# Block-diagonal fetch of the chunk inverses and 128-column streams for the small products of a hybrid DeltaNet block

## The chip, the cores and the metric

One core of a Trainium2 chip runs the whole program in one launch. The metric is the device time in microseconds (us), here the median of three runs; the profile is one further execution. The core's engines run side by side: TensorE (PE) multiplies matrices and writes PSUM, VectorE (DVE) and ScalarE (ACT) do elementwise work, GpSimd (POOL) some small operations in SBUF, and SyncE (SP) issues most transfers. PEld is PE's loading of the stationary operand.

## The reference

One transformer-like block over 1024 positions of width 1024, in float32. The part that matters here is the modulation and the chunked gated delta rule of group A, 4 heads of width 128, chunks of 64 positions:

```python
mod = (c_act @ w_ada[l] + b_ada[l])[:, None, :]
shift1, scale1, gate1, shift2, scale2, gate2 = jnp.split(mod, 6, axis=-1)
h = rms_norm(x, norm1_w[l]) * (1.0 + scale1) + shift1
...
lmat = jnp.where(strict, jnp.einsum('bhncd,bhnmd->bhncm', k_beta, k) * decay, 0.0)
tmat = lax.linalg.triangular_solve(lmat, eye, left_side=True, lower=True, unit_diagonal=True)
u = jnp.einsum('bhncm,bhnme->bhnce', tmat, v_beta)
w = jnp.einsum('bhncm,bhnmd->bhncd', tmat, k_beta * jnp.exp(g)[..., None])
```

Then a scan over the chunks, an output projection, and a SwiGLU of width 2816; the last norm ends it.

## The kernel before

The 1024 positions are two halves (`hf` 0 and 1) of 512. The first 500 us or so (input modulation, the combined projection, convolutions, the delta rule, the output projection of the first half) are written as many small tasks, and a planner (`Sim`, L298 to L523) orders their instructions while the program is built: for each instruction it estimates a start from costs (`cost`, L367; transfers from L514) and takes the earliest, with a task's priority (`PR`) breaking near ties. What it decides is the fixed order on every engine's queue; the chip only waits on data. The projection's products (`acc`) have the lowest priority and fill PE between the others. Large products are split into two parts of a rounded type (fp32r), three products each; the small ones run in plain f32, where each product leaves two records of PE in the trace. The rest of the program (from L1493) is in a written order.

Modulation: `ada0` (L625) forms shift1 and scale1 column by column. For each of 8 blocks k of 128 columns it multiplies pieces of the weights (as stationary operand) with one column of `c_act`, or sums made on DVE by `sums0` with one column of ones; `cols0` (L646) reads the result on ACT. A number of pieces per block, `N_PE`, goes to PE: 16 products for block 0, 2 or 4 for the others.

The triangular inverse: per half there are 4 heads x 4 tiles x 2 chunks, each chunk a 64x64 unit triangle. `stage_a` writes the 32x32 diagonal blocks to DRAM (`dl`); `gdn` (L1218) reads them back as 64 rows of 1024 numbers, inverts all 64 at once on DVE (the loop at L1242) and writes the inverses to DRAM (`dx`, L1247). From there ten loads bring them back in three layouts:

- `DD[:, 0]` (tile name qs): blocks stacked one under another, 32 columns wide, two loads of 64 KB on SP
- `xbd[0]` (xbd): blocks on the diagonal of a 128x128 tile for each of 16 tiles, four loads of 64 KB, each on SP or ACT as the planner chooses (`dma2`)
- `XA` (A, cleared by POOL at L1255): blocks at shifted diagonal places, four loads of 32 KB on SP or ACT

DVE turns `DD[:, 0]` round into `DD[:, 1]` (L1262), and then a `merge` (L1178) for each head makes the off-diagonal block of the 64x64 inverse: P (L1185) multiplies the off-diagonal part of L with `DD[:, 1]`, its result is copied back to `DD[:, 0]`, Q (L1192) multiplies that with `XA`, and four copies put Q into `Tt`, which also takes the turned `xbd`. With `Tt` PE forms u (L1204) and w (L1209). P and Q are two products each per head, with a moving operand of 32 columns. Then the scan over the chunks runs (products named K, A and O in the trace).

`ecopy` (L570) is a copy on ACT or DVE, whichever the planner expects to end first.

Of the kernel before, what the change touches and what calls it, by code (L numbers as in the profile page):

```python
# [12 lines left out]
AF = mybir.ActivationFunctionType  # L13
# [4 lines left out]
P = 128  # L18
# [3 lines left out]
DMA_T = (1.8, 0.9)  # L22
D = 1024
KB = 8
# [29 lines left out]
def kernel(  # L54
# [25 lines left out]
    class Ordered:  # L80
# [18 lines left out]
    PE, DVE, ACT, POOL, SP = (Ordered(n, e) for n, e in (  # L99
        ("pe", nc.tensor), ("dve", nc.vector), ("act", nc.scalar), ("pool", nc.gpsimd), ("sp", nc.sync)))  # L100
# [11 lines left out]
    xs, outs = x[0], out[0]  # L112
# [18 lines left out]
    def v3(ap, a):  # L131
        return ap.rearrange("p (a b) -> p a b", a=a)
# [7 lines left out]
    def bc1(row, n):  # L140
        return row.unsqueeze(1).to_broadcast([row.shape[0], n, row.shape[1]])
# [10 lines left out]
    ones = ones_r.bitcast(F32)  # L152
# [39 lines left out]
    def dma(out, in_):  # L192
        SP.dma_start(out=out, in_=in_)

    def dma2(out, in_):
        kw = dict(out=out, in_=in_)
        mover[0].either([("sp", "dma_start", nc.sync.dma_start, (), kw), ("act", "dma_start", nc.scalar.dma_start, (), kw)])
# [37 lines left out]
    c_act = cst.tile([P, KB], F32, name="c_act", tag="c_act")  # L235
# [13 lines left out]
    n1c, bac, n2c, gnc = cols_a[:, 0:8], cols_a[:, 8:56], cols_a[:, 56:64], cols_a[:, 64:65]  # L249
    s1c = cst.tile([P, KB], F32, name="s1c", tag="s1c")  # L250
    b1c = cst.tile([P, KB], F32, name="b1c", tag="b1c")
    nb1 = sp.tile([P, KB], F32, name="nb1", tag="nb1")
# [45 lines left out]
    class Sim:  # L298
# [187 lines left out]
        def run(self):  # L486
            while True:
                self.settle()
                best, cand = None, []
                for task in self.tasks:  # L490
                    r = task["req"]
                    if r[0] != "op":
                        continue
                    starts = [self.start_of(w) for w in r[1]]
                    r[2] = min(range(len(starts)), key=lambda i: starts[i] + r[1][i][1][2] + BIAS.get(r[1][i][0], 0.0))
                    t = starts[r[2]]
                    cand.append((prio(task), t, task["n"], r[1][r[2]], task))
                    if best is None or t < best[0]:
                        best = (t, r[1][r[2]][0])
                if best is None:  # L500
                    late_ = [x["req"] for x in self.tasks if x["req"][0] == "slot" and x["req"][1].slots]
                    if late_:
                        self.now = min(self.data_time(r[2]) for r in late_)
                        continue
                    if self.tasks:
                        raise RuntimeError("stuck: " + "; ".join(f"{x['name']}{x['args'] if x['name'] in ('gdn', 'ab_phase') else ''} {x['req'][0]} {getattr(x['req'][1], 'tag', x['req'][1])}" for x in self.tasks))
                    return
                t0, eng = best
                _, t, _, way, task = min((c_ for c_ in cand if c_[3][0] == eng and c_[1] <= t0 + HOLD.get(eng, 0.0)), key=lambda c_: c_[:3])
                outs, ins, busy, lat, table = way[1]  # L510
                if table:
                    self.table = table
                if lat is None:
                    run_ = min(n_ for n_ in (ap.ap[-1][1] * 4 for ap in outs + ins))  # L514
                    self.pipe = max(t + DMA_T[0], self.pipe) + outs[0].nbytes() / (270e3 if run_ <= 512 else 330e3 if run_ <= 1024 else 380e3)
                    end = rd = self.pipe + DMA_T[1]
                else:
                    end, rd = t + lat, t + busy + 0.1
                self.idle.setdefault(eng, []).append((self.t[eng], t, busy, task["name"], "", outs[0].tensor.name))
                self.t[eng] = t + busy  # L520
                self.now = max(self.now, t)
                self.record("dma" if lat is None else eng, outs, ins, end, rd)
                self.resume(task)  # L523
# [46 lines left out]
    def ecopy(dst, src):  # L570
        sim.either([("act", "copy", nc.scalar.copy, (dst, src), {}), ("dve", "tensor_copy", nc.vector.tensor_copy, (dst, src), {})])
# [9 lines left out]
    def mm(out_, lhsT, rhs, start=True, stop=True):  # L581
        PE.matmul(out_, lhsT, rhs, start=start, stop=stop)
# [28 lines left out]
    acs_ = {}  # L611
# [13 lines left out]
    def ada0():  # L625
        pa_ = bank(chb, "ada")
        for k in range(KB):
            sim.wait(lambda: ("wa", k) in done)
            t = wa[k]
            pa = pa_[:, 2 * k:2 * k + 2]  # L630
            sim.wait(lambda: k == 0 or k in acs_)
            n0 = KB - N_PE[k]
            for s_ in range(2):
                for kk in range(n0, KB):
                    mm(pa[:, s_:s_ + 1], t[:, kk, s_, :], c_act[:, kk:kk + 1], kk == n0, n0 == 0 and kk == KB - 1)
                if n0:
                    mm(pa[:, s_:s_ + 1], acs_[k][:, s_, :], ones[:, 0:1], n0 == KB, True)
            free(t)
            if n0:
                free(acs_[k])  # L640
            sim.spawn(cols0, PR["ada0"], k, pa)
        sim.wait(lambda: all(("cols", k) in done for k in range(KB)))
        free(pa_)
        done.add("ada0")

    def cols0(k, pa):  # L646
        ACT.activation(s1c[:, k:k + 1], pa[:, 1:2], AF.Identity, bias=nb1[:, k:k + 1], scale=n1c[:, k:k + 1])
        ACT.activation(b1c[:, k:k + 1], pa[:, 0:1], AF.Identity, bias=bac[:, k:k + 1])
        done.add(("cols", k))

# [421 lines left out]
    xbd, S = [], {}  # L1072
    sw = lambda ap: ap.rearrange("p t (c n) -> p t c n", c=2)
    tsl = lambda t: slice(t * P, (t + 1) * P)
# [103 lines left out]
    def merge(hf, h, T, XA, DD):  # L1178
        st, t_ = sc_[hf], T[h]
        u = us[hf]  # L1180
        L = t_["L"]
        sim.wait(lambda: ("a", hf, h) in done)
        pP = bank(chb, "P")
        for g in range(2):
            mm(pP[:, 32 * g:32 * g + 32], L[:, 2 * g + 1, :], DD[:, 1, 2 * h + g, :])  # L1185
        ecopy(DD[:, 0, 2 * h:2 * h + 2, :], v3(pP[:, 0:64], 2))
        free(pP)
        Tt = gt("Tt")
        DVE.transpose(flat(Tt), flat(xbd[0][:, 4 * h:4 * h + 4, :]))
        pQ = bank(chb, "Q")  # L1190
        for g in range(2):
            mm(pQ[:, 32 * g:32 * g + 32], XA[:, 2 * h + g, :], DD[:, 0, 2 * h + g, :])  # L1192
        for p in range(2):
            for c in range(2):
                q = 64 * c + 32 - 32 * p
                ecopy(Tt[64 * c:64 * c + 32, p:4:2, 64 * c + 32:64 * c + 64], v3(pQ[q:q + 32, 0:64], 2))
        free(pQ)
        done.add(("q", hf, h))
        DVE.tensor_tensor(t_["L"], t_["kt"], bc2(t_["bk"], P), ALU.mult)
        free(t_["bk"])  # L1200
        sim.wait(lambda: ("vt", hf, h) in done)
        pu = bank(chb, "u")
        for t in range(4):
            mm(pu[:, tsl(t)], Tt[:, t, :], u[:, h, t, :])  # L1204
        ecopy(flat(u[:, h]), pu)
        free(pu)
        pw = bank(chb, "w")
        for t in range(4):
            mm(pw[:, tsl(t)], t_["L"][:, t, :], Tt[:, t, :])  # L1209
        free(t_["L"])  # L1210
        free(Tt)
        ecopy(t_["WQ"].rearrange("p t (c n) -> p t c n", c=4)[:, :, 0:4:3, :],
                 pw.rearrange("p (t c n) -> p t c n", t=4, c=2))
        free(pw)
        DVE.tensor_tensor(t_["kt"], t_["kt"], bc2(st["kd"][:, :, h], P), ALU.mult)
        done.add(("uw", hf, h))

    def gdn(hf):  # L1218
# [4 lines left out]
        dx = drp.tile([64, 1024], F32, name=nm("dx"), tag="dx", bufs=2)  # L1223
# [24 lines left out]
        free(A)  # L1248
        free(tmp)
        DD = gt("qs", (P, 2, 8, 32))  # L1250
        for c in range(2):
            r0 = 32 * c + 16
            dma(DD[64 * c:64 * c + 64, 0], dx[r0:r0 + 16, :].rearrange("(h p) (a b) -> (p a) h b", p=2, a=32))
        XA = gt("A", (P, 8, P))
        POOL.memset(XA, 0.0)  # L1255
        for r in range(4):
            dma2(xbd[0][32 * r:32 * r + 32, :, 32 * r:32 * r + 32], dx[r * 16:r * 16 + 16, :].rearrange("t (a b) -> a t b", a=32))
        for c in range(2):
            for p in range(2):
                q, r0 = 64 * c + 32 - 32 * p, 32 * c + p  # L1260
                dma2(XA[q:q + 32, :, q:q + 32], dx[r0:r0 + 15:2, :].rearrange("t (a b) -> a t b", a=32))
        DVE.transpose(flat(DD[:, 1]), flat(DD[:, 0]))  # L1262
        for h in heads:
            sim.spawn(merge, PR["m"], hf, h, T, XA, DD)
# [9 lines left out]
        for t in range(4):  # L1274
# [3 lines left out]
            for cc in range(2):  # L1278
                r0 = 64 * cc
# [905 lines left out]
```

## Time and profile before

| | |
|---|---|
| runs | 1183.56, 1184.01, 1186.36 us; median 1184.01 |
| profiled execution | 1185.35 us, its span 1183.6 |
| mean granted clock of PE | 0.993 |
| POOL busy | 57.3 us of the span |
| moved by DMA | 207.58 MB, 175 GB/s mean |
| the two merges (P to Q) | from 202.3 and 390.4 us |

How to read it: the span is the time from the first to the last instruction of the profiled execution. Rows of groups give the line, engine, operation, output and inputs by tile name, shape, count, and the time spent. A row of the timeline begins with start and length in us; what stands in brackets is the idle time of that engine ahead of it and what ended it. Most small instructions are recorded with the line of a helper (L442 for all that the planner orders, L91 and L92 for the written order), so tile names are what tells them apart. In rows of stretches the columns are: stretch, its length, busy time (and number of instructions) of PE, PEld, DVE, ACT and POOL, the granted PE clock as a share of full speed, the share of the DMA engines in use, and GB/s.

### The profile page before, as it was taken

How to read it: one execution, taken by the hardware profiler on the slowest of the kernel's cores; microseconds unless marked ns; L12 is line 12 of the kernel's file. 1: busy time of each engine (PE TensorE's matmuls, PEld its weight loads, DVE VectorE, ACT ScalarE, POOL GpSimd, SP SyncE). 2: the span in 40 equal slices, each digit the busy share in tenths (PEclk: the TensorE clock that was granted, in tenths of full speed). 3: DMA queues.
4: the chain of work that ended last, by engine and by line, in shares of the span. 5: the costliest groups of instructions: out<-in, count | busy, mean ns of one | idle time of the engine just before them, and what ended most of it. 6: DMA issues, size and time to landing. Idle time of an engine off the chain costs nothing.

```text
span 1183.6 us, 16666 instructions
## 1 busy us (share of the span) xinstructions
PE 1171.5 (99%) x5657; PEld 982.9 (83%) x5657; DVE 924.8 (78%) x1720; ACT 536.3 (45%) x1174; POOL 57.3 (5%) x92
## 2 busy tenths in 40 slices
PE   8999999999999999999999999999999999999997
PEld 8888888988888888888888888888888888888886
DVE  5998888799988798758787677767767697688676
ACT  4489832458642444225443333333333365433343
POOL 2010000001100001100000000000000000000002
PEclk9999999999999899999999999999999999999999
DMA  9932456544434643722354655455644679869413
GB/s 295 291 95 64 112 161 165 177 117 136 119 103 138 158 149 140 280 86 93 133 175 133 222 190 185 145 178 187 223 152 136 221 278 395 307 202 345 146 42 142
DMA packets 179694, 207.58 MB, mean 175 GB/s; under 512 B 25749, under 2 KB 111898, under 8 KB 179610
## 3 DMA queue, kind: packets, MB, share of 16 engines
q1 hardware_dynamic: 172664, 203.16, 53.4%
q10 hardware_dynamic: 6946, 3.38, 1.1%
q8 instruction: 44, 0.72, 0.2%
q14 instruction: 40, 0.33, 0.1%
HBM read 151.44 MB, written 55.05 MB: 174 GB/s over the span
## 4 chain that ended last, share of the span: by engine, by line
PE 93%; DVE 4%; ACT 1%; DMA 1%; issue 1%; POOL 0%; ACTq 0%; DVEq 0%; POOLq 0%
PE acc L91 34%; PE acc L442 24%; PE dn L91 17%; PE o L91 4%; PE o L442 3%; PE K L442 1%; PE A L442 1%; PE u L442 1%; PE ada L442 1%; PE w L442 1%; DVE xo L92 1%; PE ab L442 1%; PE qk L442 1%; PE kk L442 1%; PE heat L91 1%
## 5 line engine op out<-in xcount | busy, mean ns | idle before, releaser
L442 PE MATMUL acc<-h,u 128*128 128x512 f32 x1200 | 303.4, 400 | 0.0
L442 PEld LDWEIGHTS acc<-h,u 128*128 128x128 f32 x1200 | 220.5, 189 | 41.8
L91 PE MATMUL acc<-h,hl 128*128 128x512 f32 x600 | 140.1, 390 | 0.0
L91 PEld LDWEIGHTS acc<-h,hl 128*128 128x128 f32 x600 | 112.4, 188 | 23.2
L91 PE MATMUL acc<-h,u 128*128 128x512 f32 x456 | 106.1, 389 | 0.0
L91 PE MATMUL acc<-T,hl 128*128 128x512 f32 x432 | 101.3, 390 | 0.2 <-ACT cc L92 0.2
L91 PEld LDWEIGHTS acc<-h,u 128*128 128x128 f32 x456 | 85.6, 188 | 17.8
L91 PEld LDWEIGHTS acc<-T,hl 128*128 128x128 f32 x432 | 80.9, 188 | 17.2 <-ACT cc L92 0.6
L92 DVE TENSOR_TENSOR xo<-xo,dn 128x512 f32<-128x512 f32 x84 | 57.1, 685 | 43.2 <-PE dn L91 34.8
L91 PE MATMUL dn<-h,h 128*128 128x512 f32 x396 | 90.7, 389 | 0.0
L92 ACT COPY cc<-acc 128x512 f32<-128x512 f32 x66 | 38.5, 591 | 108.1 <-PE acc L91 108.1
L91 PEld LDWEIGHTS dn<-h,h 128*128 128x128 f32 x396 | 74.3, 188 | 15.4
L91 PE MATMUL acc<-T,u 128*128 128x512 f32 x360 | 84.0, 389 | 0.0
L91 PEld LDWEIGHTS acc<-T,u 128*128 128x128 f32 x360 | 67.6, 188 | 14.0
L442 ACT CAST u<-raw 128x512 fp32r<-128x512 f32 x68 | 42.1, 621 | 57.0 <-PE acc L442 54.9
L92 DVE TENSOR_TENSOR cc<-cc,acc 128x512 f32<-128x512 f32 x66 | 43.8, 683 | 29.8 <-PE acc L91 29.8
L92 DVE TENSOR_TENSOR hl<-R,hl 128x512 fp32r<-128x512 f32 x60 | 39.5, 688 | 33.5 <-ACT hl L92 33.4
L442 DVE TENSOR_TENSOR u<-raw,u 128x512 fp32r<-128x512 f32 x82 | 56.2, 685 | 10.5 <-ACT u L442 10.0
L442 DVE SCALAR_TENSOR_TENSOR cv<-pr,cols_b,cv 128x512 f32<-128x512 f32 x72 | 53.0, 746 | 0.5 <-ACT cv L442 0.2
L92 ACT CAST h<-rw 128x512 fp32r<-128x512 f32 x57 | 32.7, 617 | 39.8 <-PE dn L91 34.6
L92 ACT CAST hl<-R 128x512 fp32r<-128x512 f32 x60 | 35.5, 620 | 24.0 <-DVE R L92 11.0
L92 DVE TENSOR_TENSOR u<-R,u 128x512 fp32r<-128x512 f32 x46 | 30.1, 687 | 20.5 <-ACT u L92 20.5
(344 smaller groups left out, 2020.7 us busy)
## 6 DMA issues: line engine op xcount, KB each, us to landing
raw<-in_w_in_dram SPq DMA_DIRECT2D x82, 256.0 KB, 3.4
am_scr<-cc SPq DMA_DIRECT2D x77, 256.0 KB, 4.4
raw<-in_w_ada_dram SPq DMA_DIRECT2D x56, 256.0 KB, 3.5
rw<-am_scr SPq DMA_DIRECT2D x55, 256.0 KB, 5.3
rw<-bm_scr SPq DMA_DIRECT2D x53, 256.0 KB, 5.3
bm_scr<-raw SPq DMA_DIRECT2D x51, 256.0 KB, 5.4
R<-in_w_gate_dram SPq DMA_DIRECT2D x22, 512.0 KB, 4.1
R<-in_w_up_dram SPq DMA_DIRECT2D x22, 512.0 KB, 5.4
```

The lines of the kernel that those rows point to most:

```text
L91: return call(*a, **k)
L92: ins = call(*a, **k)
L442: ins = call(*a, **k)
```

## The change

It touches four places. Modulation products and the merge's P and Q stream 128 columns instead of 1 or 32: the same numbers repeated, of which the first copy is used; P and Q of the second tile overwrite the repeats of the first. The modulation's results now take 256 PSUM columns a block, with two places used in turn. The loads of `DD` and `XA` are gone; instead, `xbd` is loaded (its rows 1 and 3 first), and its blocks are copied into `DD[:, 0]` by four copies on ACT or DVE and into `XA` by four copies on POOL. The planner's estimate of a transfer in runs of at most 128 bytes is made slower.

```diff
-                    self.pipe = max(t + DMA_T[0], self.pipe) + outs[0].nbytes() / (270e3 if run_ <= 512 else ...
+                    self.pipe = max(t + DMA_T[0], self.pipe) + outs[0].nbytes() / (150e3 if run_ <= 128 else 270e3 if run_ <= 512 else ...
...
-            pa = pa_[:, 2 * k:2 * k + 2]
+            pa = pa_[:, k % 2 * 256:k % 2 * 256 + 256]
...
-                    mm(pa[:, s_:s_ + 1], t[:, kk, s_, :], c_act[:, kk:kk + 1], kk == n0, n0 == 0 and kk == KB - 1)
+                    mm(pa[:, tsl(s_)], t[:, kk, s_, :], c_act[:, kk:kk + 1].to_broadcast([P, P]), kk == n0, n0 == 0 and kk == KB - 1)
                 if n0:
-                    mm(pa[:, s_:s_ + 1], acs_[k][:, s_, :], ones[:, 0:1], n0 == KB, True)
+                    mm(pa[:, tsl(s_)], acs_[k][:, s_, :], ones, n0 == KB, True)
...
-        ACT.activation(s1c[:, k:k + 1], pa[:, 1:2], AF.Identity, bias=nb1[:, k:k + 1], scale=n1c[:, k:k + 1])
+        ACT.activation(s1c[:, k:k + 1], pa[:, P:P + 1], AF.Identity, bias=nb1[:, k:k + 1], scale=n1c[:, k:k + 1])
...
-            mm(pP[:, 32 * g:32 * g + 32], L[:, 2 * g + 1, :], DD[:, 1, 2 * h + g, :])
+            mm(v3(pP[:, 32 * g:32 * g + P], 4), L[:, 2 * g + 1, :], bc1(DD[:, 1, 2 * h + g, :], 4))
...
-            mm(pQ[:, 32 * g:32 * g + 32], XA[:, 2 * h + g, :], DD[:, 0, 2 * h + g, :])
+            mm(v3(pQ[:, 32 * g:32 * g + P], 4), XA[:, 2 * h + g, :], bc1(DD[:, 0, 2 * h + g, :], 4))
...
         DD = gt("qs", (P, 2, 8, 32))
-        for c in range(2):
-            r0 = 32 * c + 16
-            dma(DD[64 * c:64 * c + 64, 0], dx[r0:r0 + 16, :].rearrange("(h p) (a b) -> (p a) h b", p=2, a=32))
         XA = gt("A", (P, 8, P))
         POOL.memset(XA, 0.0)
-        for r in range(4):
+        for r in (1, 3, 0, 2):
             dma2(xbd[0][32 * r:32 * r + 32, :, 32 * r:32 * r + 32], dx[r * 16:r * 16 + 16, :].rearrange("t (a b) -> a t b", a=32))
-        for c in range(2):
-            for p in range(2):
-                q, r0 = 64 * c + 32 - 32 * p, 32 * c + p
-                dma2(XA[q:q + 32, :, q:q + 32], dx[r0:r0 + 15:2, :].rearrange("t (a b) -> a t b", a=32))
+        for p in range(2):
+            for c in range(2):
+                q = 64 * c + 32
+                ecopy(DD[64 * c + 32 * p:64 * c + 32 * p + 32, 0], xbd[0][q:q + 32, p::2, q:q + 32])
+        for p in range(2):
+            for c in range(2):
+                q, r = 64 * c + 32 - 32 * p, 64 * c
+                POOL.tensor_copy(XA[q:q + 32, :, q:q + 32], xbd[0][r:r + 32, p::2, r:r + 32])
         DVE.transpose(flat(DD[:, 1]), flat(DD[:, 0]))
```

More of the change, by code (lines that the diff above doesn't have):

```diff
@@ L514, in run @@
                     run_ = min(n_ for n_ in (ap.ap[-1][1] * 4 for ap in outs + ins))
-                    self.pipe = max(t + DMA_T[0], self.pipe) + outs[0].nbytes() / (270e3 if run_ <= 512 else 330e3 if run_ <= 1024 else 380e3)
+                    self.pipe = max(t + DMA_T[0], self.pipe) + outs[0].nbytes() / (150e3 if run_ <= 128 else 270e3 if run_ <= 512 else 330e3 if run_ <= 1024 else 380e3)
                     end = rd = self.pipe + DMA_T[1]
```

## The prediction

> **What bounds the kernel now.** I read the page's first two parts, then who TensorE (PE) waited for, then stretches of the time with the granted clock.
>
> ```profile
> PE 1171.5 (99%) x5657; PEld 982.9 (83%) x5657; DVE 924.8 (78%) x1720; ACT 536.3 (45%) x1174; POOL 57.3 (5%) x92
> ...
> PE   8999999999999999999999999999999999999997
> ...
> PEclk9999999999999899999999999999999999999999
> ```
>
> ```profile
> PE ps L91 <- POOL ghl L92: 2.5, 1, 2.5
> PE P L442 <- DVE ch L442: 1.5, 1, 1.5
> PE tr L442 <- DVE hf L442: 0.6, 1, 0.6
> PE o L442 <- DVE wu L442: 0.2, 1, 0.2
> ```
>
> PE is the bound: 99% busy, and between the start and the tail its waits are 1.5 + 0.6 + 0.2 and a few tenths. Other engines matter only where they make PE wait, so there are two ways to win: fewer or shorter PE cycles, or a faster PE clock. Nearly all slices have the full clock; one shows 8. I cut finer there and at the other merge (the columns: stretch, PE busy, PEld busy, DVE, ACT, POOL, clock, DMA share, GB/s):
>
> ```profile
> 202.18:205.59 3.41, 3.41 (x31) 3.33 (x29) 3.30 (x6) 1.47 (x8) 0.00 (x0) 1.00 0.71 223
> 205.59:212.41 6.82, 6.82 (x31) 6.53 (x30) 6.79 (x12) 3.52 (x15) 1.47 (x2) 0.50 0.58 187
> 212.41:215.83 3.42, 3.42 (x32) 3.42 (x32) 1.83 (x3) 1.85 (x4) 0.00 (x0) 1.00 0.59 192
> 389.90:393.32 3.42, 2.96 (x25) 2.81 (x25) 3.42 (x9) 2.21 (x7) 0.00 (x0) 1.00 1.01 295
> 393.32:400.15 6.83, 6.83 (x30) 6.45 (x30) 5.87 (x12) 4.43 (x18) 0.95 (x1) 0.50 0.17 53
> ...
> 11.03:14.44 3.41, 3.41 (x34) 3.41 (x32) 0.81 (x2) 0.32 (x1) 0.70 (x2) 1.00 1.10 313
> ```
>
> Twice the clock is halved for 6.8 us, although PE was busy for all of the 3.41 us before the first dip. What ran there:
>
> ```profile
> 202.35 1.86 PE L442 MATMUL P<-qs,L 128*128 128x32 f32 x16
> 204.05 0.47 PE L442 MATMUL acc<-h,u 128*128 128x512 f32 x1
> 204.36 2.33 PE L442 MATMUL Q<-qs,A 128*128 128x32 f32 x16
> ...
> 210.06 1.91 PE L442 MATMUL w<-Tt,L 128*128 128x128 f32 x8
> ...
> 213.20 1.06 PE L442 MATMUL w<-Tt,L 128*128 128x128 f32 x8
> ```
>
> Before each dip stand the 32-column products P and Q of a merge, and hardly anything else: these are the narrowest streams after the start. From 212.41 to 215.83 PE ran only the 128-column products u and w, of the same weight loads and type, and the clock was back and stayed. So I read the dips as the answer to a PE that streams few columns per load, not to an idle PE.
>
> **The change, part by part.**
>
> (1) P and Q widened to 128 columns. If the dips go, 6.82 + 6.83 us at half clock shrink. At half clock at most half of that is lost, 6.8 in all; by the w group, 1.91 against 1.06, it is (1 - 1.06/1.91) x 13.65 = 6.1. I take **-6.4**; the ends are 0 (dips stay) and -6.8. PE is busy through both dips, so the time is PE's own.
>
> (2) What the wider streams cost. A call leaves two records: 64 for P and Q, 76 for the modulation.
>
> ```profile
> 12.38 3.41 PE L442 MATMUL ada<-c_act,wa 128*128 128x1 f32 x30
> ...
> 15.90 1.50 PE L442 MATMUL heat<-ident,ones 128*128 128x128 f32 x12
> ...
> 21.32 0.28 PE L442 MATMUL ada<-ones,ac 128*128 128x1 f32 x2
> ...
> 25.73 0.38 PE L442 MATMUL ada<-ones,ac 128*128 128x1 f32 x2 [0.17 <-DVE ac L442]
> ```
>
> ```profile
> L442 PE MATMUL ada<-c_act,wa x48: 164/250/250, 10.6 to 46.7; 128*128 128x1 f32 x48
> ...
> L442 PE MATMUL ada<-ones,ac x28: 164/250/271, 21.3 to 52.5; 128*128 128x1 f32 x28
> ...
> L442 ACT ACTIVATE s1c<-ada,nb,cols_a x8: 330/352/353, 15.8 to 53.1; 128x1 f32<-128x1 f32 x8
> ```
>
> With a last record of 0.25 taken off, 1-column records follow each other every (3.41 - 0.25)/29 = 0.109 us, 32-column ones (P) every (1.86 - 0.25)/15 = 0.107, 128-column ones (heat) every (1.50 - 0.25)/11 = 0.114: the weight load sets the pace, not the columns. Cost: 76 x 0.005 + 64 x 0.007 = **+0.8**. No row has a repeated (broadcast) moving operand; if it streamed at half rate, 128 columns would take as long as 256, and by the 512-column group
>
> ```profile
> 380.72 8.09 PE L442 MATMUL acc<-h,u 128*128 128x512 f32 x35
> ```
>
> (8.09 - 0.25)/34 = 0.23 per 512, that is 0.115 for 256, still the weight load's pace. The bounds are 0 and +1.0. The 1-column modulation run (11.03 to 14.44) caused no dip in this execution, so widening that part gets no gain from me. Its bank halves are now reused every second block: product k+2 waits for ScalarE's two reads of block k, but the products of one block and the next stand some 4 us apart (21.32, 25.73), which hides two reads of 0.35 or less; with that cover gone it would be 0.7 a block.
>
> (3) The DMA route. Per merge ten loads become four; gone are two of 64 KB into DD (qs) and four of 32 KB into XA (A), on SP and ACT. This is what stood in front of the second merge:
>
> ```profile
> 379.62 0.49 SPq L442 DMA_DIRECT2D dx<-A  x1
> ...
> 383.45 0.32 ACTq L442 DMA_DIRECT2D xbd<-dx  x1
> 383.49 1.29 SPq L442 DMA_DIRECT2D qs<-dx  x2
> ...
> 387.16 1.41 ACTq L442 DMA_DIRECT2D A<-dx  x2
> ...
> 388.61 0.62 ACT L442 CAST h<-raw 128x512 fp32r<-128x512 f32 x1 [4.48 <-DMA xbd<-dx]
> ...
> 389.26 0.69 DVE L442 TENSOR_TENSOR h<-raw,h 128x512 fp32r<-128x512 f32 x1 [2.88 <-ACT h L442]
> 389.87 0.43 DVE L442 STREAM_TRANSPOSE qs<-qs 128x256 f32<-128x256 f32 x1
> ```
>
> ACT's cast stood behind ACT's own two XA loads, DVE's subtraction behind the cast, the transpose behind the subtraction, and P behind the transpose: PE idled 1.54 until 390.36, having run out at 388.82. The change takes those loads out of ACT's and SP's queues. Instead: xbd rows 1 and 3 are issued first, four DD copies of 32x256 follow on ACT or DVE, then the transpose. Prices:
>
> ```profile
> L442 ACT COPY Tt<-Q x31: 198/203/207, 204.9 to 396.7; 32x64 f32<-32x64 f32 x31
> ```
>
> ```profile
> L442 ACT COPY qs<-A x13: 579/582/584, 230.0 to 450.5; 64x512 f32<-64x512 f32 x13
> ```
>
> ```profile
> DMA to landing us min/median/max: 3.0/3.2/4.1
> ```
>
> The last row is that of the xbd loads. A copy of 256 elements lies between the two copy rows: 0.20 + 192/448 x 0.38 = 0.36, so 0.7 for four on two engines (1.45 on one). From 383.5: 3.2 + 0.3 issue + 0.7 + 0.43 = 388.1 (up to 389.8 with landing 4.1 and one engine). PE is there at 388.82 in the old order, so the wait of 1.54 goes: **-1.5**, ends -1.9 and +1.0. If the copies queue behind an ACT cast as before, P is late again.
>
> Q needs XA, now four POOL copies of 256 elements after rows 0 and 2 have landed; no trace row shows one. The nearest:
>
> ```profile
> L442 POOL TENSOR_TENSOR rk<-nk,nhalf 128x4 f32<-128x4 f32 x8 | 9.3, 1157 | 102.7 <-DVE nk L442 63.4 <-DVE egl L442 39.3
> L442 POOL MEMSET A<- 128x1024 f32 x4 | 3.8, 957 | 119.7 <-DMA dx<-A 99.4 <-PE Q L442 20.2
> ...
> L442 POOL TENSOR_SCALAR st<-st 128x1 f32<-128x1 f32 x8 | 3.2, 402 | 83.0 <-ACT jk L442 57.2 <-ACT raw L442 25.7
> L442 POOL MEMSET A<- 64x512 f32 x6 | 3.1, 522 | 86.2 <-PE O L442 86.2
> ```
>
> The memsets give 0.435 per 512 elements, so 0.3 for 256 as the low end; a TENSOR_SCALAR that reads and writes has a floor of 0.40, plus 0.22 for the elements: 0.62, which I take; the high end is the 1.16 of the power. Four: 2.5 (1.2 to 4.6). Beside it run the DD copies, the transpose and P (0.7 + 0.43 + 1.86 = 3.0), which hide it; without that cover Q waits up to 1.6 a merge. I put 0. [...]
>
> (4) Plan. The order is made anew from the planner's estimates, now slower for runs of 128 bytes and less; every instruction after the first such load can change place. Nothing in the trace prices that; the rows are PE's waits above. I add one small new wait each at the start and at a merge, together **+0.7** (the size of the 0.64 row), ends -0.4 and +4.
>
> Sum: -6.4 + 0.8 - 1.5 + 0.7 = **-6.4**. The profiled execution has a span of 1183.6 and a time of 1185.35, so 1179.0 there; the median shown is 1184.01, so **1177.6**. It would come as shorter stretches around 205 and 393; the rest stays PE's.
>
> **Rivals.**
>
> *The dips stay* (the change doesn't do what it says). The gate might count something that widening doesn't change. For it: the 1-column run at 11.03 to 14.44, with (14.44 - 12.38)/0.109 = 19 of 34 records narrow, brought no dip, so narrowness alone is not proven. Against: u and w at 128 columns ran at full clock for a whole such stretch, and what remains different in the merges is width. Time: 1184.0 + 0.8 - 1.5 = 1183.3. [...]
>
> *The second merge takes back the first dip.* PE reaches it 3.2 us earlier, and the triangular solve on DVE doesn't. DVE is 78% busy over the span, and its solve is followed by a fixed path of dx, landing and transpose; for it speaks that PE waited there already. Against: DVE's order is mixed with evacuations of PE's banks, so it moves up with PE, and the plan knows nothing of the dips, so their going brings PE nearer to the plan. -6.4 + 3.2 + 0.8 = -2.4, if the queue jam also remains: 1181.6.
>
> [...]
>
> **Chances.** Forecast 0.66 (own range 1174.5 to 1180.4), dips stay 0.12, given back at the second merge 0.13, Q behind POOL 0.09. A measurement here tells 0.3% (3.6 us) from no change: the forecast is faster, the next two are same, the last is slower. Range 1174.5 to 1185.0: from all terms at their good end (-6.8 - 1.9 - 0.4) to past the first two rivals; a tenth lies above, a little below.
>
> **What would show it.** Right: a clock of 1.00 through both merges; P and Q as 128x128 records about 0.11 apart; no PE wait of over 1 us at P or Q; no loads into qs or A from dx, and the four POOL copies at about 0.6. Wrong in part: a stretch of 6.8 us at 0.50 after a merge (term 1), spacing near 0.2 in P, Q or ada (term 2), PE waiting at P for DVE (term 3) or at Q for POOL (the last rival), new waits elsewhere (term 4). The prediction falls if both dips stay, or if PE's waits grow by more than 4 us.

## The result and the profile after

The changed kernel takes 1179.2 us (median of 6 runs, 1177.95 to 1180.71) against 1184.0 for the kernel before (6 runs, 1181.99 to 1186.36): a ratio of 0.9957 with a 95% interval of 0.9943 to 0.9971, so 0.43% faster. The profiled execution has a span of 1178.9 where it was 1183.6. The first two parts of the page of the changed kernel:

```profile
PE 1167.2 (99%) x5657; PEld 976.9 (83%) x5657; DVE 927.2 (79%) x1724; ACT 536.0 (45%) x1179; POOL 57.2 (5%) x100
...
PEclk9999999999999999999999999999999999999999
```

The slice with an 8 is gone. Stretches of 3.4 us, half as long as a dip of the kernel before, over the two merges of the changed kernel (stretch, length, busy PE, PEld, DVE, ACT, POOL, clock, DMA share, GB/s), and the first P and Q that PE ran in them:

```profile
212.42:215.83 3.41, 3.41 (x31) 3.36 (x30) 3.41 (x6) 1.54 (x8) 0.00 (x0) 1.00 0.87 280
215.83:219.24 3.41, 3.41 (x30) 3.28 (x29) 3.41 (x7) 3.13 (x15) 1.47 (x2) 1.00 0.43 115
393.00:396.40 3.40, 2.92 (x24) 2.70 (x24) 3.40 (x7) 1.87 (x6) 0.50 (x1) 1.00 0.70 198
396.40:399.80 3.40, 3.40 (x29) 3.27 (x29) 3.40 (x7) 3.15 (x15) 0.95 (x1) 1.00 0.56 155
```

```profile
212.42 1.95 PE L442 MATMUL P<-qs,L 128*128 128x128 f32 x16
...
214.44 1.95 PE L442 MATMUL Q<-qs,A 128*128 128x128 f32 x16
```

Full clock all through, and (1.95 - 0.275)/15 = 0.112 us from record to record: four times the columns at the same pace. Whom PE waited for in the changed kernel (total, times, longest):

```profile
PE ps L91 <- POOL wab L92: 2.3, 1, 2.3
PE tr L91 <- DVE x L442: 1.0, 2, 0.9
PE tr L442 <- DVE hf L442: 0.7, 1, 0.7
PE P L442 <- DVE qs L442: 0.5, 1, 0.5
```

The wait at P fell from 1.5 to 0.5, none is at Q, and a new one of 1.0 stands at the transposes (tr) that follow the planned part. To see where the 4.7 us of span went I take first starts of four groups, from each one's row of its tile; of the kernel before:

```profile
L442 PE MATMUL heat<-ident,ones x36: 275/275/356, 9.3 to 17.1; 128*128 128x128 f32 x36
...
L442 PE MATMUL pt<-ident,raw x1: 267/267/267, 54.4 to 54.4; 60*128 60x60 f32 x1
...
L91 PE MATMUL o<-L,WQ x32: 390/393/481, 490.0 to 530.3; 128*128 128x512 f32 x32
...
L91 PE MATMUL acc<-T,hl x432: 389/389/500, 553.2 to 966.8; 128*128 128x512 f32 x144
```

and of the changed kernel:

```profile
L442 PE MATMUL heat<-ident,ones x36: 273/275/275, 9.6 to 17.5; 128*128 128x128 f32 x36
...
L442 PE MATMUL pt<-ident,raw x1: 268/268/268, 55.0 to 55.0; 60*128 60x60 f32 x1
...
L91 PE MATMUL o<-L,WQ x32: 389/392/477, 483.9 to 525.8; 128*128 128x512 f32 x32
...
L91 PE MATMUL acc<-T,hl x432: 389/389/499, 548.7 to 962.4; 128*128 128x512 f32 x144
```

| from, to | before | after | difference |
|---|---|---|---|
| span's start to heat (planned) | 9.3 | 9.6 | +0.3 |
| heat to pt (modulation) | 45.1 | 45.4 | +0.3 |
| pt to the late projection o (both merges) | 435.6 | 428.9 | -6.7 |
| o to the T products of the SwiGLU | 63.2 | 64.8 | +1.6 |
| T products to the end | 630.4 | 630.2 | -0.2 |

So 6.7 us were won where the dips and the wait at P had been, and 1.6 were lost again behind the planned part, of which PE's waits at tr are 1.0. The timeline of the changed kernel at that place (start, length, then in brackets the idle time before):

```profile
482.55 3.56 SPq L442 DMA_DIRECT2D x_scr<-x  x4
...
493.98 3.67 DVE L442 SCALAR_TENSOR_TENSOR x<-x,st,u 128x1024 f32<-128x1024 f32 x3 [1.35 <-DMA x_scr<-x]
...
496.52 0.33 PE L91 MATMUL tr<-ident,x 128*128 128x128 f32 x1 [0.16 <-DVE x L442]
497.71 1.64 PE L91 MATMUL tr<-ident,x 128*128 128x128 f32 x13 [0.87 <-DVE x L442]
```

DVE scales x in place and must wait until its stores have read it; PE wants the scaled x at 496.0 and gets the last at 497.7. In the kernel before the stores were issued only 1.1 us later (483.62), but PE came to its transposes 6.1 us later (502.05), so this path had slack.

Last, the new copies in the changed kernel, by tile (ns, least, median, most), with the landing of the loads in front of them, and rows of the timeline at the first merge and in front of P of the second:

```profile
L442 POOL COPY A<-xbd x8: 387/397/906, 208.7 to 392.7; 32x256 f32<-32x256 f32 x8
...
L442 ACT COPY qs<-xbd x7: 400/403/404, 207.0 to 391.3; 32x256 f32<-32x256 f32 x7
...
DMA to landing us min/median/max: 3.7/4.2/5.0
```

```profile
209.34 1.64 POOL L442 COPY A<-xbd 32x256 f32<-32x256 f32 x3 [0.24 <-DMA xbd<-dx]
209.94 0.78 DVE L442 TENSOR_TENSOR u<-raw,u 128x512 fp32r<-128x512 f32 x1
...
210.64 0.88 DVE L442 SCALAR_TENSOR_TENSOR aacc<-raw,c_act,aacc 128x512 f32<-128x512 f32 x1
...
389.95 1.78 ACT L442 COPY qs<-xbd 32x256 f32<-32x256 f32 x4 [0.43 <-DMA xbd<-dx]
391.76 1.14 ACT L442 CAST u<-raw 128x512 fp32r<-128x512 f32 x2
392.41 0.84 DVE L442 TENSOR_TENSOR u<-raw,u 128x512 fp32r<-128x512 f32 x1 [0.83 <-ACT u L442]
393.17 0.43 DVE L442 STREAM_TRANSPOSE qs<-qs 128x256 f32<-128x256 f32 x1
393.65 2.05 PE L442 MATMUL P<-qs,L 128*128 128x128 f32 x16 [0.48 <-DVE qs L442]
```

A POOL copy takes 0.40 alone and up to 0.91 beside DVE; DVE's own two instructions took 0.78 and 0.88 at the first merge where their kind takes 0.69 and 0.75. PE never waited for a POOL copy itself. The 0.48 that it still waited at the second P end in a chain of the old kind: all four DD copies ran on ACT, ACT's cast stood behind them, DVE's subtraction behind the cast, and the transpose behind the subtraction. That subtraction ran beside POOL and took 0.84 in place of 0.69.

### The profile page after: what moved, and what is told of

Read it like the earlier page. It is cut to its first block, busy times and chain, and to the rows that moved or that the text cites. A ratio compares the mean times of both kernels' runs of the same rounds, so it can differ in the third digit from the quotient of the medians.

```text
span 1178.9 us, 16679 instructions
## 1 busy us (share of the span) xinstructions
PE 1167.2 (99%) x5657; PEld 976.9 (83%) x5657; DVE 927.2 (79%) x1724; ACT 536.0 (45%) x1179; POOL 57.2 (5%) x100
## 4 chain that ended last, share of the span: by engine, by line
PE 91%; DMA 4%; DVE 2%; SPq 1%; ACT 1%; issue 1%; ACTq 0%; DVEq 0%
PE acc L91 34%; PE acc L442 24%; PE dn L91 17%; PE o L91 3%; PE o L442 3%; SPq L442 1%; PE A L442 1%; PE K L442 1%; DMA x_scr<-x 1%; DMA raw<-in_w_ada_dram 1%; DVE xo L92 1%; PE ab L442 1%; PE kk L442 1%; PE ada L442 1%; PE w L442 1%
## 5 line engine op out<-in xcount | busy, mean ns | idle before, releaser
L442 PE MATMUL acc<-h,u 128*128 128x512 f32 x1200 | 298.1, 397 | 0.0
L91 PE MATMUL acc<-h,u 128*128 128x512 f32 x456 | 106.1, 389 | 0.0
L442 ACT CAST u<-raw 128x512 fp32r<-128x512 f32 x64 | 39.6, 622 | 59.6 <-PE acc L442 57.2
```

What stands on the lines that cost most here:

```text
L91: return call(*a, **k)
L442: ins = call(*a, **k)
```

## Experiments

All times are medians of runs that alternate with the kernel before on the same chip, which took 1184.4, 1184.6 and 1183.4 in the three groups; ratios are to these. "Narrow" means 1 or 32 columns, "wide" 128, and a dip is a stretch at half clock. "The gate" in the texts of the runs is whatever halves the clock: the traces show the clock that was granted, 1.00 or 0.50, and not what decides over it.

**1. Only P and Q widened; only the modulation widened.** Both keep every engine's order of before.

```diff
-            mm(pP[:, 32 * g:32 * g + 32], L[:, 2 * g + 1, :], DD[:, 1, 2 * h + g, :])
+            mm(v3(pP[:, 32 * g:32 * g + P], 4), L[:, 2 * g + 1, :], bc1(DD[:, 1, 2 * h + g, :], 4))
...
```

> The kernel before with nothing but P and Q of the merges streamed as 128 columns; the order of every engine's instructions is the one of before. Theory (few streamed columns per weight load bring the half clock): no stretch at 0.50 after either merge, mean granted clock 0.999; -6.1 to -6.8 for the dips and +0.45 for the width, so 1178.0, if the wait of 1.5 at the second P does not grow; a longer wait there (up to 4.7, if DVE's solve sets that point) gives 1181. Rival 1 (the dips come from something else in the merges, for example the burst of loads or the wait): both dips stay, 1184.4. Rival 2 (the gain of the change is the new plan and the route, not the width): 1184.

> The kernel before with nothing but the modulation products streamed as 128 columns, same order. Theory: 76 records at 0.005 more each, +0.4, both dips stay: 1184.4. Rival (the narrow modulation run sometimes brings a dip of its own at the start, depending on where the gate's stretches lie): some runs up to 3 us faster, and the spread of the runs is smaller than the 4 us of before.

P and Q alone: 1181.55, ratio 0.9968 (0.9955 to 0.9981), where I had expected 1178.0. The modulation alone: 1184.9, ratio 1.0004 (0.9992 to 1.0015), as expected. The trace of the first held a surprise; stretches of it, the first at the start of the kernel, the last over its first merge:

```profile
11.93:15.34 3.41, 3.41 (x34) 3.41 (x32) 0.90 (x2) 0.83 (x1) 0.00 (x0) 1.00 1.14 319
15.34:22.16 6.82, 6.82 (x30) 6.43 (x31) 5.54 (x11) 2.12 (x4) 0.00 (x0) 0.50 1.13 309
...
195.00:235.00 40.00, 40.00 (x254) 35.84 (x254) 33.47 (x64) 16.95 (x45) 2.96 (x4) 1.00 0.65 185
```

The merges are at full clock, as the theory has it, and the wait at the second P was 1.6, not 4.7. But here the narrow modulation run at the start brought a dip, in a part whose code and order are those of the kernel before, where there had been none. Its seven runs fall into two by the mean clock: 1179.05 and 1179.23 at 0.999, and 1181.2 to 1182.22 at 0.995 to 0.997. So the dip comes and goes: a narrow place is halved in some executions and not in others. The start dip costs less than a merge dip: heat to pt takes 56.6 - 9.6 = 47.0 in this trace against 45.1, so 1.9. In the trace of the second kernel a merge's dip lasted longer than any before:

```profile
390.00:400.00 10.00, 10.00 (x47) 9.52 (x47) 8.41 (x15) 5.95 (x23) 0.95 (x1) 0.54 0.38 116
400.00:410.00 10.00, 10.00 (x75) 9.52 (x74) 6.68 (x11) 6.08 (x12) 0.00 (x0) 0.95 0.57 174
```

(0.46 + 0.05) x 10 / 0.5 = 10.2 us at half clock: three times 3.41. In the 3.41 before it PE had idled 1.7, waiting at P. The first merge's dip of the same trace lasted only 3.41 (206.48 to 209.89).

**2. The route alone; the changed kernel with narrow P and Q.** The first is the kernel before with the new loads, copies and planner price; the second undoes the two lines of experiment 1 in the changed kernel. Both have the changed kernel's order.

> The kernel before with the new route only (xbd loaded, copies into DD and XA on chip, slower planner price for short runs); P, Q and the modulation stay narrow. Its order is that of the changed kernel. Theory: both dips stay at 0.50 for 6.8 us each, the wait at the second P is at most 0.5; the plan's give-back around 497 is smaller since PE comes there later: 1183 to 1184.5. Rival (the route and plan bring the gain): 1179 to 1180 with no dips.

> The changed kernel with P and Q back at 32 columns, the modulation still at 128, same order as the changed kernel. Theory: the dips are back after both merges; about 6.4 - 0.4 slower than the changed kernel less what it gives back around 497 (1.0), so 1184. Rival (route or plan removed the dips): 1178.8, no dips.

Route alone: 1182.28, ratio 0.9980 (0.9968 to 0.9991), a little less than the 1183 to 1184.5 that I had expected with both dips. Changed kernel with narrow P and Q: 1180.41, 0.9971 (0.9958 to 0.9984), but with runs from 1178.95 to 1185.89. I had expected 1184 there; the profiled execution shows why it was less. Its two merges and their stretches:

```profile
212.22 1.87 PE L442 MATMUL P<-qs,L 128*128 128x32 f32 x16
...
214.24 1.87 PE L442 MATMUL Q<-qs,A 128*128 128x32 f32 x16
```

```profile
195.00:235.00 40.00, 40.00 (x242) 35.45 (x241) 34.24 (x68) 19.87 (x52) 4.49 (x8) 1.00 0.60 175
380.00:410.00 30.00, 30.00 (x190) 26.93 (x189) 25.88 (x48) 21.66 (x52) 4.40 (x6) 1.00 0.80 219
```

Narrow products, no dip: this execution was lucky twice. What such luck is made of can be read from where dips start. In the trace of the route alone:

```profile
15.21:22.03 6.82, 6.82 (x31) 6.53 (x31) 4.88 (x11) 2.12 (x4) 0.00 (x0) 0.50 1.16 315
...
397.50:404.33 6.83, 6.83 (x31) 6.54 (x31) 4.94 (x10) 4.40 (x18) 0.95 (x1) 0.50 0.40 115
```

There is one dip at the start and one after the second merge, none after the first. Their starts are 382.29 us apart, 112 times 3.413; in the kernel before it is 187.73 (205.59 to 393.32), 55 times, and with the modulation wide 184.32 (206.48 to 390.80), 54 times. So in each of these three executions the two dips start a whole number of steps of 3.413 us apart (382.29/112, 187.73/55 and 184.32/54 all give it, and 6.83 is two), as on a grid. Where such a grid lies in the program is not the same in all: counted back in these steps, the first planned heat product starts 1.6 after one in the kernel before (9.26) and 1.2 after one with the modulation wide (9.7). In the lucky execution only PE's idle end is at half clock; if the grid holds there too, counting back 281 such steps from its start gives the stretches over the first merge:

```profile
211.00:214.41 3.41, 3.41 (x27) 3.12 (x25) 3.13 (x6) 1.47 (x5) 0.03 (x1) 1.00 0.91 278
214.41:217.83 3.42, 3.42 (x29) 3.30 (x29) 3.42 (x7) 2.81 (x14) 1.47 (x2) 1.00 0.47 152
...
1173.56:1177.60 4.04, 0.00 (x0) 0.00 (x0) 0.40 (x1) 0.37 (x1) 0.00 (x0) 0.50 0.52 192
```

P (from 212.22) and Q (from 214.24) fall into two stretches, each with more than 1 us of wide products beside them; in the kernel before, the one stretch from 202.18 to 205.59 held all of P and half of Q. This fits both outcomes, but no run here sets the place of such a grid, so it is not shown that this alone decides. The two executions also price a dip, since their order is the same: from pt to o the route takes 431.4 (56.7 to 488.1) with one merge dip and a wait of 0.4 at P, the lucky one 427.9 (54.7 to 482.6) with neither.

So "narrow" makes a dip possible, not certain, and one look at one execution cannot tell whether the width matters. The runs of the kernel before say the same. Of 56 of them, by mean granted clock (6.83 us at half clock lower the mean by 3.41/1184 = 0.003):

| mean clock | runs | median us |
|---|---|---|
| 0.996 | 13 | 1181.9 |
| 0.994, 0.995 | 11 | 1183.9 |
| 0.993 | 18 | 1184.6 |
| 0.991, 0.992 | 14 | 1186.0 |

The six runs of the changed kernel read 0.998 or 0.999, short of 1 because PE's idle end is at half clock too (0.50 for the last 3.1 us of the profiled span, 1175.81 to 1178.93). All 56 lie below that, so each has had a dip. The profiled execution, at 0.993, was an ordinary one.

**3. Chance taken out.** To make a dip certain I gave the merges a long narrow stretch: P and Q issued three times over (the repeats write the same numbers), the modulation wide, and the same instructions in the same order at 32, 64 and 128 columns.

```diff
         for g in range(2):
-            mm(pP[:, 32 * g:32 * g + 32], ...)
+            for _ in range(3):
+                mm(pP[:, 32 * g:32 * g + 32], ...)
...
```

> The kernel before with the modulation at 128 columns and each of P and Q issued three times over at 32 columns (the repeats write the same numbers), so that the narrow stretch of a merge lasts some 11 us and must cover whole stretches of the gate wherever they lie. Theory: half clock after both merges in every run, for longer than 6.8 us, since the first stretch at half clock is narrow again; 64 calls more at 0.22 = 14 us, or 0.4 each where the clock is halved, so 1184.4 + 14 + 4 to 8 = 1202 to 1206; all runs within 3 us. Rival (the width doesn't matter): the same time as the 128-column twin.

> The twin of the three-fold narrow kernel with the same instructions in the same order, P and Q at 128 columns. Theory: no dip, 1179.3 + 14 + 0.9 = 1194, that is 8 to 12 us less than the narrow twin though it streams four times as many columns. Rival (the width doesn't matter): within 1 us of the narrow twin, or slower by the 0.9 of the width.

> The three-fold P and Q with 64 columns, same order as the 32- and 128-column twins (1200.7 and 1193.3). Theory, if the gate counts streamed columns per time: a record each 0.11 us streams 64 columns in about 0.026, a share of a quarter against an eighth at 32 and a half at 128; the half clock fell at up to about a sixth so far. So no dip and 1193.0 if the threshold lies below a quarter; 1200 if it lies above. Rival (only a full 128 columns counts as busy): 1200.

| columns | median us (4 runs) | lowest and highest | ratio to before, interval |
|---|---|---|---|
| 32 | 1200.66 | 1200.32, 1201.23 | 1.0133 (1.0119 to 1.0146) |
| 64 | 1192.58 | 1192.31, 1194.07 | 1.0078 (1.0061 to 1.0094) |
| 128 | 1193.3 | 1192.96, 1193.58 | 1.0069 (1.0054 to 1.0084) |

The 64-column twin ran in another group than the other two, so its ratio is the better figure. Stretches of the narrow twin over its merges:

```profile
205.40:215.30 9.90, 9.90 (x61) 9.90 (x61) 8.21 (x13) 3.12 (x11) 0.00 (x0) 0.66 0.38 116
388.84:392.25 3.41, 3.41 (x33) 3.41 (x32) 1.91 (x3) 1.54 (x4) 0.00 (x0) 1.00 0.93 293
392.00:404.00 12.00, 12.00 (x65) 12.00 (x65) 5.87 (x11) 5.33 (x15) 0.00 (x0) 0.57 0.41 133
```

PE is busy in every microsecond, also in the 3.41 before the second dip, so no idle gap brings the half clock; (0.34 x 9.90 + 0.43 x 12)/0.5 = 17 us lie at half clock, 8.5 lost at most, and the twin with four times the columns is 7.4 faster. All four runs of each agree within 1.8 us and have the same mean clock, 0.991 and 0.999: with a long enough stretch, chance is out. I had expected 8 to 12, so the gain came a little small. Width, and nothing else, is what these three kernels differ in; at 64 columns the clock was kept as at 128, at a mean of 0.999 in all four runs.

**4. What the route and the planner's price are worth.** The kernel before with all products wide (old loads, old order), and the changed kernel with the old price:

```diff
-outs[0].nbytes() / (150e3 if run_ <= 128 else 270e3 if run_ <= 512 else ...
+outs[0].nbytes() / (270e3 if run_ <= 512 else ...
```

> The kernel before with P, Q and the modulation all at 128 columns, loads and order as before. Theory now (each of three narrow places brings a half-clock stretch of 6.8 us, 3.3 us lost, in those runs in which it covers one of the gate's 3.41 us stretches; the width alone carries the change's gain): no dips at any of the three, mean clock 0.998 or 0.999 in every run, spread under 3 us, the first late projection product (o from L91) at 483.5, median 1179.3; the wait of 1.6 at the second P stays. Rival (route and plan are needed for a part of the gain): 1181 with no dips.

> The changed kernel with the planner's old price for short runs, so another order; widths and route as in the changed kernel. Theory: no dips; the 1.6 us that the changed kernel loses between the late projection and the first SwiGLU products belongs to its plan, so another plan may lose 0 to 2: 1177.5 to 1180. Rival (the price is what keeps the merges free of waits): over 1.5 us of waits at P or Q and 1181.

All wide, old route: 1181.0, ratio 0.9965 (0.9953 to 0.9978). That is the number of the rival, not of the theory (1179.3). One of its five runs read a mean clock of 0.996 where I had expected 0.998 or more in each; it was no longer than the others (1180.84), and there is no trace of it, so wide products are not shown to rule out every dip. Its waits and the late projection:

```profile
PE P L442 <- DVE ch L442: 1.5, 1, 1.5
PE Q L442 <- DMA A<-dx: 0.8, 1, 0.8
```

```profile
L91 PE MATMUL o<-L,WQ x32: 390/393/475, 485.6 to 525.9; 128*128 128x512 f32 x32
```

With pt at 55.2, pt to o is 430.4: 5.2 less than before, which is the two dips (6.4) less a new wait of 0.8 at Q for the XA loads and 0.3 for the width. The old route, then, costs 2.3 of waits at P and Q in this order; the changed kernel waits 0.5 there.

Old price, new route: 1176.66, ratio 0.9931 (0.9919 to 0.9944), the fastest version of all and below the 1177.5 to 1180 that I had expected. Waits and the same two rows of its trace:

```profile
PE A L442 <- DVE S L442: 0.6, 1, 0.6
```

```profile
L91 PE MATMUL o<-L,WQ x32: 389/393/477, 481.6 to 521.8; 128*128 128x512 f32 x32
...
L91 PE MATMUL acc<-T,hl x432: 389/389/500, 544.7 to 958.3; 128*128 128x512 f32 x144
```

No wait at P or Q, and 63.1 from o to T, as before: neither the wait at P of 0.5 nor the 1.6 lost behind the planned part is there. Both came with the price. Its span is 4.0 shorter than the changed kernel's: 1.4 of this lies between pt and o and 1.7 between o and T (0.2 more go to heat to pt), but 1.1 lies before heat (8.5 against 9.6), where two executions of one order differ as much (8.6 and 9.6 in the changed order with P and Q narrow and wide). Is a higher price worse, or was this plan a bad draw? Two more prices, and the old price with all products narrow:

> The changed kernel with a planner price of 200 in place of 150 for runs of at most 128 bytes (old: 270). Theory (the price only reshuffles the plan, and the changed kernel's plan happens to be a poor one at the norm of the second half): no dips, anywhere from 1176 to 1180, without order in the price. Rival (a higher price makes the plan steadily worse): between 1176.7 and 1179.2.

> The changed kernel with a planner price of 120. Theory (reshuffling): anywhere from 1176 to 1180. Rival (a price nearer to the measured transfers is steadily worse): above 1179.2.

> The new route at the planner's old price, all products narrow as before; same order as the version that ran at 1176.66. Theory: the three places bring half-clock stretches again by chance, 0 to 3 a run, 3.3 us for a merge and some 1.9 for the start, so runs from 1176 to 1183, median 1180.5; the width is worth about 3.5 to 4 in this plan too. Rival (the widths don't matter in a plan without the wait at P): 1176.5.

| price for short runs | ratio to before, interval |
|---|---|
| 120 | 0.9952 (0.9939 to 0.9965) |
| 150 (the change) | 0.9957 (0.9943 to 0.9971) |
| 200 | 0.9972 (0.9961 to 0.9984) |
| 270 (old) | 0.9931 (0.9919 to 0.9944) |

The time rises from 120 to 200 and falls at 270 (1177.86, 1179.2, 1180.36, 1176.66 us), so it does not simply follow the price. I read it so that each price draws another plan, and plans differ by up to 4 us; four prices cannot show more. At 200 the time was a little outside what I had allowed (1180), at 120 well below the rival's bound. Old price, narrow: 1178.95, ratio 0.9957 (0.9942 to 0.9972), runs from 1176.21 to 1181.38; expected 1180.5. The lowest runs equal those of the wide twin, the highest lie 4.7 above. Its trace has two dips of 3.41, one at the start and one after the first merge: the lottery again.

## Why the prediction was right, and where it was off

The forecast was 1177.6 in a range of 1174.5 to 1185.0, faster at 0.66; measured 1179.2. The direction and the main cause held: in the profiled pair both dips went. Part of the closeness is luck, since the sum was built on one execution that happened to have two dips, where others of the same kernel have fewer or more, and terms that were too large and too small offset each other. The sizes, term by term:

**Term 1, the dips (-6.4).** The cause was right: the three twins show it with all else equal, at a mean clock of 0.991 with 32 columns and 0.999 with 64 and with 128. In the profiled pair the size was nearly right too: pt to o lost 6.7, of which the wait at P is 1.0, so 5.7 are left, or 6.0 with the 0.3 that the width of P and Q costs there. Mis-sized was its weight in the medians: I took the dips of one execution for those of all. Widening everything with the old order gave 0.35% of 1184.6, 4.1 us; widening at the changed kernel's order gave 0.9980 to 0.9957, 2.7; at the old price 0.9957 to 0.9931, 3.1. By their mean clock, the 56 runs reach from about one dip of 6.8 to nearly three.

**Term 2, the width (+0.8).** Right: +0.3 to +0.4 from heat to pt (45.4 and 45.5 in the changed kernel and in the one with only the modulation wide, against 45.1), and 64 x (0.112 - 0.107) = 0.3 at P and Q. The repeated operand streams at the pace of any other (0.112 against 0.114 for heat). Wrong was "widening that part gets no gain from me": in other executions the modulation run does bring a dip, worth 1.9. The 1-column run without a dip, which I had counted for the rival, was luck.

**Term 3, the route (-1.5).** The wait at P fell from 1.5 to 0.5, so -1.0. Three things in front of P were off: the xbd loads landed after 4.2 where the old row had 3.2, the four copies ran on ACT alone in 1.78 (I had 0.7 on two engines, 1.45 on one), and the transpose stood behind DVE's subtraction and ACT's cast, the queue that the prediction had named as the way to be late again. The POOL copies took 0.55 on average where I had 0.62, and Q did not wait. DVE's instructions beside them took about 0.1 longer, which the sum had put at nothing; at the second merge 0.15 of it lay on the way to P. Three POOL copies of 0.76 to 0.91 began during a DVE instruction with two SBUF inputs, and each ended 0.25 to 0.26 after that instruction; the other five took 0.39 to 0.40. What held the three up is not settled by so few. What I had not foreseen is a gain: without the dips the old route made Q wait 0.8 for XA.

**Term 4, the plan (+0.7).** Too small: +1.6 behind the planned part in the changed kernel, of which 1.0 are waits at tr and the rest is not explained. It is the term with the widest ends, and rightly so.

**The rivals.** "The dips stay" fell with the twins. "The second merge takes back the first dip" fell with the wait at the second P, 1.6 when only P and Q were widened and 1.5 with everything wide and no dip at all: the solve on DVE moved up with PE. "Q behind POOL" fell: no wait at Q, with copies of 0.55 on average and 0.91 at most. (The lower end of the range, 1174.5, should read 1174.9 by its own terms; nothing hangs on it.)

What adds up: with everything wide, the new route and its plan bring 0.9965 to 0.9957, within the intervals nothing; at the old price they bring 0.9965 to 0.9931, 4 us. I read the change as a whole as the width's gain plus a route whose gain its own plan mostly spent. How much of the 4 us is the route and how much a lucky plan at the old price is not separated; the waits of 2.3 at P and Q are the part that the traces show.

## What to carry to other kernels

Look at the granted clock in stretches of a few microseconds, not only at busy time: a PE that is 100% busy on narrow products can run at half speed (0.50 for 6.82 us after 3.41 us without a gap), and widening them with repeated columns costs next to nothing where, as here, records of 1 and of 128 columns follow each other at nearly the same pace (0.109 and 0.114 us). Before one execution's dip is put into a sum, see how often it falls: the mean clock of every run tells of it, and an experiment that makes the narrow stretch long takes the chance out. Where a planner orders the program, a change to its prices is a new draw of the whole order, worth up to 4 us here; try the change with the old prices too.

## What the hardware showed that I had not expected

- The half clock came also where PE had not idled at all in the 3.41 us before, at the first merge of the kernel before and at both of the narrow twin. It lasted 3.41 us times a whole number: 6.8 in six of the dips seen, 3.4 in three, 10.2 in two (with only the modulation wide, and in the narrow twin). The starts of two dips in one execution lie 54, 55 and 112 such steps apart. Steps that run free of the program would explain why the same place is halved in one execution and not in the next; that is my reading, which no run here tests.
- What halves the clock is not settled. 64 columns a record kept it (a mean of 0.999) and 32 did not (0.991). At 0.23 per 512 columns I estimate 22% of the stretch 202.18 to 205.59 as streaming, with a dip after it, and 19% of 11.03 to 14.44, without one. That speaks against a plain count of streamed columns but does not exclude it, because one 512-column product at the edge of a stretch is 7% of it. The same pace gives 0.029 for 64 columns: the 0.026 in the text of that run stands in no row, but the share of a record of 0.11 is about a quarter with either; and its "up to about a sixth" is 22% by this count.
- Records of 1, 32 and 128 columns in plain f32, each with a weight load of its own, followed each other every 0.109, 0.107 and 0.114 us, and repeated ones of 128 every 0.112. For 64 columns there is the time of the run alone: the 64-column twin ran at 1192.58 and the 128-column one at 1193.3, so 0.7 us apart for 192 records, and by ratio (1.0078 and 1.0069) not apart at all.
